# Retention's sample values by a transfer instead of a selector product, and layer norms that take the moments first

## The chip, the core and the metric

The kernel runs on one core of a Trainium2 chip as one program. Its time is the device time in microseconds (us), given as the median of several runs. The engines named below are TensorE (PE, with PEld for its weight loads), VectorE (DVE), ScalarE (ACT), GpSimd (POOL) and SyncE (SP). Every transfer between the chip's DRAM and its on-chip memory is issued by SP, in the order of the program, and is carried by the 16 DMA engines that all transfers share.

## The reference, cut to what matters

Two decoder layers work on one prompt (16 learned meta tokens and 256 tokens) and on 8 samples of one token each. In each layer three mixers (Mamba-2, HGRN2, retention) read one projection, their outputs are merged by gates, and layer norms and a SwiGLU follow. The parts that matter here are the retention step of the samples and the layer norm:

```
new_state = state * gamma(h) + k (outer) v        # per sample and head: 256 x 512
o         = q @ new_state
mu  = mean(x);  var = mean((x - mu)^2);  y = (x - mu) * rsqrt(var + eps) * g + b
```

There are 4 heads and 8 samples, so 32 such states in a layer and 64 in all. Each state is read from DRAM, updated and written back (512 KB each way).

## The kernel before

Features lie on the 128 partitions and the 280 tokens (272 of the prompt, 8 samples) along the free dimension. All large products go through blocks of 128 output features: `wblock` (L204) loads 512 KB of weights into one of 3 `raw` buffers, ACT rounds them to `wh`, and DVE computes the remainder `wl` (4 buffers each). 24 matmuls (L160, `large`) then make one block in PSUM tile `pp`. Small products (L169, `mm`) are placed between them: generators of the mixers are advanced one step by `tick()` twice in a block, so the order of the work on each engine is fixed when the program is built, and every engine runs its own queue in that order. SP's queue is one of these: a transfer that must wait holds up all those behind it.

The samples' retention is `ret_samples` (L753). The generator runs beside the later projections of its layer, one sample in a step. A step does the following:

- PE makes the output products of the sample before (`po<-st`, 8 matmuls).
- SP loads the state into one of 3 `st` buffers, and ACT multiplies it by gamma (L769).
- PE fetches the values: `vb` (L771) is a product of a selector column, broadcast over 128 columns, with `vhl`, which holds the samples' values as two rounded parts on 96 partitions. It puts the 512 values of sample b on all 128 partitions of a PSUM bank.
- DVE adds k times `vb` to the state in two instructions (`st<-vb`), and SP stores the state (L774).

Mamba and HGRN2 already hand their samples' values on in another way. They store them as rows in DRAM, and `everywhere` (L613) loads rows with a stride of 0 over the partitions, into tile `vh` (4 buffers, 256 KB a load).

A layer norm takes the sums by products with 1/1024 (`onesd`); `inv_std` then computes the inverse deviation, and `scaled` multiplies, applies gain and bias, and splits x into `px` tiles. `opening` (L228) starts the next projection: three blocks at once, which begin with those parts of x that are ready. `less(j)` subtracts the mean from quarter j of x. At the start `ln_input` does the same for the input, while the first weights arrive. The last norm writes the result, `yT`.

Of the kernel before, what the change touches and what calls it, by code (L numbers as in the profile page):

```python
# [8 lines left out]
F32 = mybir.dt.float32  # L9
# [6 lines left out]
P = 128  # L16
L = 2

OPEN = 3
# [69 lines left out]
def body(ctx: ExitStack, tc: tile.TileContext, a: dict):  # L89
# [113 lines left out]

    def wblock(src, nk):  # L204

        src_ = wraw.tile([P, RC, P], F32, tag="raw", name="raw")
        load(out=src_[:, :nk, :], in_=src)
        hi = whp.tile([P, RC, P], F32R, tag="wh", name="wh")
        lo = wlp.tile([P, RC, P], F32R, tag="wl", name="wl")
        with tc.high_priority(offset=boost):  # L210
            copy(hi[:, :nk, :], src_[:, :nk, :])
            ins = sub(lo[:, :nk, :], src_[:, :nk, :], f32(hi[:, :nk, :]))
        if fence:
            nosync(raw(ins), fence.pop())
        return hi, lo
# [9 lines left out]

    opened, norm_end = [], []

    def opening(srcs, c0):  # L228

        ps = [pp.tile([P, 512], F32, tag="pp", name="pp")[:, c0:T] for _ in srcs]  # L230
        ws = [wblock(src, KB) for src in srcs]
        for j in range(4):
            for p, w in zip(ps, ws):
                for k in (2 * j, 2 * j + 1):
                    for part in w:
                        large(p, part[:, k, :], blk(xhl[0], k)[:, c0:T], k == 0 and part is w[0], False)
        for j in range(3):
            for p, w in zip(ps, ws):
# [5 lines left out]
        opened.extend(ps)  # L244
        fence[:] = norm_end

# [110 lines left out]
    def scaled(x, rs, gk, bk, vec, less):  # L357
# [22 lines left out]
        with tc.high_priority(offset=AHEAD):  # L380
            vec(mul(x[0][:, 0, c], x[0][:, 0, c], rs))
            upper(0, V)
            vec(mul(x[0][:, 1, c], x[0][:, 1, c], rs))
            upper(1, S)
            times(1)
            upper(2, S)
# [33 lines left out]
    def ln_input(x):  # L420
# [4 lines left out]
        mm(m1, first, x[0][:, 0, :], True, True)  # L425
        for j in range(4):
            sub(x[j], x[j], b2(m1))
            sq = pair("pm")
            S.activation(sq, x[j], AF.Square)
            if j % 2:  # L430
                total = pair("pm")
                add(total, x[j - 1], x[j])
                for i in range(2):
                    ins = mm(mu, onesd, total[:, i, :], j == 1 and i == 0, j == 3 and i == 1)
            if j < 3:
                add(sq[:, 0, :], sq[:, 0, :], sq[:, 1, :])
                mm(m2, onesd, sq[:, 0, :], j == 0, False)
            else:
                for i in range(2):
                    ins = mm(m2, onesd, sq[:, i, :], False, i == 1)  # L440
        keep_warm(14, ins)
        rs = tt_()
        scaled(x, rs, "lnin_g", "lnin_b", *inv_std(rs, mu, m2, x))

    def inv_std(rs, mu, m2, x):
# [4 lines left out]
        def less(j):  # L450
            vec(sub(x[j][:, :, c], x[j][:, :, c], b2(mu)))

        with tc.high_priority(offset=AHEAD):
            S.activation(rs, mu, AF.Square)
            less(0)
            vec(sub(rs, m2, rs))
            vec(V.tensor_scalar(rs, rs, 0.0, None, ALU.max))
            rstd_of(rs, rs, 1.0, 0)
            less(1)
        return vec, less  # L460

    class Residual:
# [37 lines left out]
        def norm(self, gk, bk, out=None):  # L500
# [5 lines left out]
            for j in range(4):  # L506
                x = self.x[j]
                if j > 1:
                    less(j)
                vec(mul(x[:, :, c], x[:, :, c], b2(rs)))  # L510
                for i in range(2):
                    ins = affine(x[:, i, c], x[:, i, c], gk, bk, 2 * j + i, S if i else V)
                    if i == 0:
                        vec(ins)
                store(out=out[j], in_=x[:, :, c])
# [22 lines left out]
    V.tensor_copy(negb, negm)  # L538
    selb = cst.tile([P, 8], F32R, name="selb")
    V.tensor_copy(selb, small[:, 24:32])  # L540
    selh = cst.tile([P, 16], F32R, name="selh")
# [71 lines left out]
    def everywhere(rows, bb):  # L613

        vb = flat("vh")
        load(out=vb, in_=rows[2 * bb:2 * bb + 2, :].rearrange("b q -> (b q)").unsqueeze(0).to_broadcast([P, 512]))
        return vb
# [26 lines left out]
    def ret_mix(l, h, proj, res):  # L644
# [24 lines left out]

        vhl = flat("vh", dt=F32R)  # L670
        vt = []
        for t0, n in TOK:
# [3 lines left out]
            if n < P:  # L676
                copy(vhl[0:32], ps[0:32, :])
                sub(vhl[32:64], ps[0:32, :], f32(vhl[0:32]))
                V.tensor_copy(vhl[64:96], f32(vhl[0:32]))
            else:  # L680
                hi, lo = flat("pm", dt=F32R), flat("pm", dt=F32R)
# [39 lines left out]

        res += y, vhl, qk, final
        sq = []
# [28 lines left out]

    def ret_samples(l, h, y, vhl, qk, ready):  # L753
        gam = 1.0 - 2.0 ** (-5.0 - h)
# [9 lines left out]
        for b in range(NS):  # L764
            yield 1
            if b:
                products(b - 1)
            st = state(a["s_ret"][l, h, b], "p (i q) -> p i q", i=2)
            S.activation(st, st, AF.Copy, scale=gam)  # L769
            vb = vbt()  # L770
            mm(vb, selb[0:96, b:b + 1].to_broadcast([96, P]), vhl[0:96, :], True, True)  # L771
            for i in range(2):
# [881 lines left out]
```

## Time and profile before

| | us |
|---|---|
| median of 3 runs | 1899.39 (1896.95 to 1900.35) |
| profiled execution, its time | 1897.69 |
| profiled execution, its span | 1895.6 |
| PE busy | 1827.3 |
| DVE busy | 1353.2 |
| ACT busy | 1090.3 |

The span is what the trace covers of the profiled execution. Samples' retention lies at about 396 to 640 us in layer 0 and at 1340 to 1580 us in layer 1. The norms lie at the start, at about 750, 961 and 1682 us, and at the end. A tile's name in a row stands for all its buffers; `out<-in` says what an instruction writes and reads.

### The profile page before, as it was taken

How to read it: one execution, taken by the hardware profiler on the slowest of the kernel's cores; microseconds unless marked ns; L12 is line 12 of the kernel's file. 1: busy time of each engine (PE TensorE's matmuls, PEld its weight loads, DVE VectorE, ACT ScalarE, POOL GpSimd, SP SyncE). 2: the span in 40 equal slices, each digit the busy share in tenths (PEclk: the TensorE clock that was granted, in tenths of full speed). 3: DMA queues.
4: the chain of work that ended last, by engine and by line, in shares of the span. 5: the costliest groups of instructions: out<-in, count | busy, mean ns of one | idle time of the engine just before them, and what ended most of it. 6: DMA issues, size and time to landing. Idle time of an engine off the chain costs nothing.

```text
span 1895.6 us, 38951 instructions
## 1 busy us (share of the span) xinstructions
PE 1827.3 (96%) x15744; PEld 1702.4 (90%) x15744; DVE 1353.2 (71%) x2183; ACT 1090.3 (58%) x1861; POOL 374.6 (20%) x415
## 2 busy tenths in 40 slices
PE   8989999999999999999999889999999999999997
PEld 7987788899888999999999778888988999999997
DVE  7898879766755766655478979996767567666654
ACT  6686677545555544544366857775455556454443
POOL 2032424211011023000220333342110100221001
PEclk9999999999999999999999989999999999999998
DMA  6545655556788744555545356555667886545563
GB/s 208 184 141 199 214 203 175 199 203 224 244 282 285 278 167 147 176 170 173 170 139 184 112 198 226 186 192 204 204 227 263 296 306 229 181 149 189 180 175 103
DMA packets 114995, 378.42 MB, mean 200 GB/s; under 512 B 13056, under 2 KB 18560, under 8 KB 114816
## 3 DMA queue, kind: packets, MB, share of 16 engines
q1 hardware_dynamic: 114816, 375.94, 59.1%
q8 instruction: 124, 2.03, 0.4%
q14 instruction: 55, 0.45, 0.1%
HBM read 317.61 MB, written 58.28 MB: 198 GB/s over the span
## 4 chain that ended last, share of the span: by engine, by line
PE 78%; DVE 11%; ACT 4%; DMA 3%; issue 2%; POOL 2%; DVEq 0%; ACTq 0%; POOLq 0%; SPq 0%
PE pp L160 63%; PE mx L169 9%; PE po L169 2%; PE vb L169 2%; DVE wl L142 2%; DVE pm L142 2%; DMA st<-s_ret 1%; DVE pa L142 1%; POOL hpt L142 1%; DMA ret_s<-st 1%; DVE py L154 1%; PE mx L172 1%; ACT wh L139 1%; DVE st L154 1%; DVE py L142 1%
## 5 line engine op out<-in xcount | busy, mean ns | idle before, releaser
L160 PE MATMUL pp<-px,wh 128*128 128x280 f32 (+1 forms) x5504 | 1119.0, 295 | 11.9 <-ACT pa L1090 5.7
L160 PEld LDWEIGHTS pp<-px,wh 128*128 128x128 f32 x5504 | 889.0, 190 | 29.8 <-issue 14.8
L142 DVE TENSOR_TENSOR wl<-raw,wh 128x1024 fp32r<-128x1024 f32 (+1 forms) x472 | 590.7, 1253 | 331.8 <-ACT wh L139 327.6
L160 PE MATMUL pp<-px,wl 128*128 128x280 f32 (+1 forms) x2752 | 796.7, 291 | 0.0
L139 ACT ACTIVATE wh<-raw 128x1024 fp32r<-128x1024 f32 (+1 forms) x472 | 493.8, 1048 | 349.8 <-PE pp L160 239.3
L160 PEld LDWEIGHTS pp<-px,wl 128*128 128x128 f32 x2752 | 521.9, 190 | 4.3 <-issue 0.8
L160 PE MATMUL pp<-py,wh 128*128 128x280 f32 (+1 forms) x1984 | 383.4, 289 | 0.8 <-ACT py L139 0.8
L160 PEld LDWEIGHTS pp<-py,wh 128*128 128x128 f32 x1984 | 313.7, 188 | 3.8 <-ACT py L139 1.3
L160 PE MATMUL pp<-py,wl 128*128 128x280 f32 (+1 forms) x992 | 285.2, 288 | 0.0
L160 PEld LDWEIGHTS pp<-py,wl 128*128 128x128 f32 x992 | 186.6, 188 | 0.7
L142 POOL TENSOR_TENSOR pa<-pa 128x280 f32<-128x280 f32 (+3 forms) x56 | 75.2, 1353 | 362.3 <-DVE pa L142 257.1
L169 PE MATMUL mx<-pm 128*32 128x16 f32 (+8 forms) x1728 | 116.6, 231 | 8.2 <-POOL pm L142 6.9
L769 ACT ACTIVATE st<-st 128x1024 f32<-128x1024 f32 x64 | 67.8, 1059 | 94.9 <-DMA st<-s_ret 62.7
L169 PEld LDWEIGHTS mx<-pm 128*32 128x32 f32 (+2 forms) x1728 | 87.5, 131 | 29.6 <-POOL pm L142 7.5
L154 DVE SCALAR_TENSOR_TENSOR st<-vb,qks,st 128x512 f32<-128x512 f32 x128 | 91.2, 745 | 23.7 <-PE vb L169 23.2
L142 DVE TENSOR_TENSOR pm<-pm 128x64 f32<-128x64 f32 (+7 forms) x179 | 85.9, 502 | 14.5 <-ACT pm L736 8.4
L142 DVE TENSOR_TENSOR pa<-pa,pp 128x280 f32<-128x280 f32 (+1 forms) x152 | 65.9, 433 | 37.0 <-PE pp L160 25.3
L142 POOL TENSOR_TENSOR pa<-px 128x560 f32<-128x560 f32 (+1 forms) x16 | 25.4, 1586 | 305.0 <-DVE py L142 304.8
L132 ACT ACTIVATE pm<-pm 128x544 f32<-128x544 f32 (+4 forms) x112 | 58.0, 540 | 13.2 <-DVE pm L154 13.1
L132 ACT ACTIVATE pa<-pp 128x280 f32<-128x280 f32 (+1 forms) x124 | 47.3, 385 | 28.8 <-PE pp L160 28.7
L139 ACT ACTIVATE pa<-pp 128x280 f32<-128x280 f32 (+1 forms) x80 | 31.4, 392 | 39.7 <-PE pp L160 39.6
L154 DVE SCALAR_TENSOR_TENSOR st<-vh,qks,st 128x128 f32<-128x128 f32 x128 | 39.7, 370 | 19.5 <-POOL st L142 11.7
(252 smaller groups left out, 1871.9 us busy)
## 6 DMA issues: line engine op xcount, KB each, us to landing
raw<-w_in SPq DMA_DIRECT2D x256, 512.0 KB
raw<-w_ffn_in SPq DMA_DIRECT2D x88, 512.0 KB
st<-s_ret SPq DMA_DIRECT2D x64, 512.0 KB
ret_s<-st SPq DMA_DIRECT2D x64, 512.0 KB
vh<-rows SPq DMA_DIRECT2D x64, 256.0 KB
raw<-w_br_r SPq DMA_DIRECT2D x32, 512.0 KB
raw<-w_ffn_out SPq DMA_DIRECT2D x32, 512.0 KB
st<-s_ssm SPq DMA_DIRECT2D x16, 512.0 KB
```

What stands on the lines that cost most here:

```text
L132: ins = S.activation(out, in_, func, **kw)
L139: return S.activation(out, in_, AF.Copy)
L142: return e.tensor_tensor(out, x, y, op)
L154: return V.scalar_tensor_tensor(out, x, s, y, op0, op1)
L160: place[0] = raw(TE.matmul(out, lhsT, rhs, start=start, stop=stop, skip_group_check=True))
L169: return put(TE.matmul(out, lhsT, rhs, start=start, stop=stop, skip_group_check=True))
L172: return put(TE.transpose(out, x, ident))
L769: S.activation(st, st, AF.Copy, scale=gam)
```

## The change

A head's values of the samples are now copied on ACT from PSUM into two `pq` tiles and stored as 8 rows of 512 in DRAM (`vrows`, 2 buffers). In each step `everywhere` loads one row to all partitions, into the 4 `vh` buffers, and DVE reads it there. The selector product is gone. `vhl` stays for the prompt's products but moves to the tile `pb`, which has one buffer.

In the norms `less(0)` and `less(1)` move behind the computation of the variance: before, the DVE subtracted the mean from x[0] ahead of it. `ln_input` issues its steps in another order, loads the first three weight blocks there and ties two of their copies behind the last square (and one behind the inverse deviation). The last norm puts nearly all of its gain and bias on ACT.

```diff
@@ wblock
-            copy(hi[:, :nk, :], src_[:, :nk, :])
+            ins = copy(hi[:, :nk, :], src_[:, :nk, :])
+            if behind_ is not None:
+                nosync(raw(ins), raw(behind_))
@@ opening
-        ws = [wblock(src, KB) for src in srcs]
+        ws = ahead or [wblock(src, KB) for src in srcs]
@@ scaled
             upper(1, S)
+            less(1)
             times(1)
@@ ln_input
+        centre(0)
+        centre(1)
+        mean(0)
+        centre(2)
+        centre(3)
+        squares(0)
+        mean(1)
+        squares(1)
+        squares(2)
...
+        ahead.extend(wblock(a["w_in"][0, b], KB, last_sq) for b in range(OPEN - 1))
         keep_warm(14, ins)
...
+        how = inv_std(rs, mu, m2, x)
+        fence[:] = norm_end
+        ahead.append(wblock(a["w_in"][0, OPEN - 1], KB, run["ops"][-1]))
+        scaled(x, rs, "lnin_g", "lnin_b", *how)
@@ inv_std
             S.activation(rs, mu, AF.Square)
-            less(0)
             vec(sub(rs, m2, rs))
             vec(V.tensor_scalar(rs, rs, 0.0, None, ALU.max))
             rstd_of(rs, rs, 1.0, 0)
-            less(1)
+            norm_end[:] = [less(0)]
@@ Residual.norm
-                if j > 1:
-                    less(j)
                 vec(mul(x[:, :, c], x[:, :, c], b2(rs)))
+                if j < 3:
+                    less(j + 1)
                 for i in range(2):
-                    ins = affine(x[:, i, c], x[:, i, c], gk, bk, 2 * j + i, S if i else V)
...
+                    ins = affine(x[:, i, c], x[:, i, c], gk, bk, 2 * j + i, V if i == 0 and j == 3 else S)
@@ everywhere
-        load(out=vb, in_=rows[2 * bb:2 * bb + 2, :].rearrange("b q -> (b q)").unsqueeze(0).to_broadcast([P, 512]))
+        n = 512 // rows.shape[1]
+        load(out=vb, in_=rows[n * bb:n * bb + n, :].rearrange("b q -> (b q)").unsqueeze(0).to_broadcast([P, 512]))
@@ ret_mix
-        vhl = flat("vh", dt=F32R)
+        vhl = flat("pb", dt=F32R)
+        rows = dr.tile([NS, 512], F32, tag="vrows", name="vrows")
...
+                for i in range(2):
+                    vs, c = flat("pq", 256), slice(256 * i, 256 * i + 256)
+                    copy(vs[0:32], ps[0:32, c])
+                    store(out=rows[:, c], in_=vs[24:32])
@@ ret_samples
             st = state(a["s_ret"][l, h, b], "p (i q) -> p i q", i=2)
+            vb = everywhere(rows, b)
             S.activation(st, st, AF.Copy, scale=gam)
-            vb = vbt()
-            mm(vb, selb[0:96, b:b + 1].to_broadcast([96, P]), vhl[0:96, :], True, True)
```

The scheduler places the instructions anew. On SP's queue, in the last head of layer 0, one finds before (`st` loads from `s_ret`, `raw` are weight blocks, `ret_s` the stores of states; the numbers name single buffers' contents):

```order
L587 DMA st_7393<-s_ret 128x1024
L207 DMA raw_7424<-w_in 128x1024
L774 DMA ret_s<-st_7202 128x1024
L207 DMA raw_7478<-w_in 128x1024
L587 DMA st_7458<-s_ret 128x1024
L207 DMA raw_7511<-w_in 128x1024
L774 DMA ret_s<-st_7258 128x1024
L207 DMA raw_7555<-w_in 128x1024
L587 DMA st_7545<-s_ret 128x1024
```

And at the same head now (`vh` loads the values of a sample from `vrows`):

```order
L605 DMA st_7419<-s_ret 128x1024
L635 DMA vh_7421<-vrows_6021 128x512
L207 DMA raw_7450<-w_in 128x1024
L605 DMA st_7484<-s_ret 128x1024
L635 DMA vh_7486<-vrows_6021 128x512
L798 DMA ret_s<-st_7419 128x1024
L207 DMA raw_7504<-w_in 128x1024
L207 DMA raw_7537<-w_in 128x1024
L798 DMA ret_s<-st_7484 128x1024
L605 DMA st_7571<-s_ret 128x1024
L635 DMA vh_7573<-vrows_6021 128x512
```

Before, a state's store stood two loads behind its own load; now it stands one load behind it, and a values' load stands behind each state's load.

On DVE, in the norm at the start (`x0` is x, `tt` the variance and then the inverse deviation, `mx_107` the mean, `lbt`, `negb`, `selb`, `selh` and `wdt` are constants), there stood before:

```order
L142 TENSOR_TENSOR wl_241<-raw_238,wh_240 128x1024
L142 TENSOR_TENSOR x0_87<-x0_87,mx_107 128x560
L142 TENSOR_TENSOR tt_153<-mx_108,tt_153 128x280
L538 CAST negb_209<-negm_203 128x288
L457 TENSOR_SCALAR tt_153<-tt_153 128x280
L142 TENSOR_TENSOR x0_88<-x0_88,mx_107 128x560
L142 TENSOR_TENSOR wl_247<-raw_244,wh_246 128x1024
L142 TENSOR_TENSOR wl_253<-raw_250,wh_252 128x1024
L142 TENSOR_TENSOR x0_87<-x0_87,tt_153 128x280
L878 CAST wdt_230<-tt_353 128x8x16
L343 TENSOR_SCALAR px_162<-x0_87,par_95 128x280
```

And now:

```order
L142 TENSOR_TENSOR wl_147<-raw_144,wh_146 128x1024
L556 CAST identb_225<-ident_215 128x128
L142 TENSOR_TENSOR tt_165<-mx_108,tt_165 128x280
L142 TENSOR_TENSOR lbt_244<-par_95,lbt_244 128x8 x2
L479 TENSOR_SCALAR tt_165<-tt_165 128x280
L142 TENSOR_TENSOR x0_87<-x0_87,mx_107 128x560
L558 CAST negb_227<-negm_221 128x288
L560 CAST selh_229<-small_219 128x16
L142 TENSOR_TENSOR x0_87<-x0_87,tt_165 128x280
L346 TENSOR_SCALAR px_179<-x0_87,par_95 128x280
L142 TENSOR_TENSOR x0_87<-x0_87,tt_165 128x280
L142 TENSOR_TENSOR x0_88<-x0_88,mx_107 128x560
```

Two `wl` stood between the variance and the product of x[0] with the inverse deviation. Now they stand ahead of the variance, and the third (`wl_176`) follows on the last row shown, ahead of the product for x[1].

## Rows read from the trace of the kernel before

**Rows 1.** the page: busy time by engine, then the chain that ended last, by line
```profile
PE 1827.3 (96%) x15744; PEld 1702.4 (90%) x15744; DVE 1353.2 (71%) x2183; ACT 1090.3 (58%) x1861; POOL 374.6 (20%) x415
...
PE pp L160 63%; PE mx L169 9%; PE po L169 2%; PE vb L169 2%; DVE wl L142 2%; DVE pm L142 2%; DMA st<-s_ret 1%; DVE pa L142 1%; POOL hpt L142 1%; DMA ret_s<-st 1%; DVE py L154 1%; PE mx L172 1%; ACT wh L139 1%; DVE st L154 1%; DVE py L142 1%
```

**Rows 2.** windows, retention's samples: us; PE, PEld, DVE, ACT, POOL; PEclk, DMA share, GB/s
```profile
396.00:500.00 104.00, 102.54 (x791) 93.22 (x791) 70.99 (x107) 57.36 (x97) 10.60 (x13) 1.00 0.66 226
500.00:640.00 140.00, 137.26 (x1088) 124.41 (x1088) 85.47 (x107) 75.11 (x102) 14.88 (x10) 1.00 0.83 289
1340.00:1440.00 100.00, 97.86 (x769) 89.10 (x768) 67.61 (x105) 52.58 (x90) 12.29 (x16) 1.00 0.65 221
1440.00:1580.00 140.00, 139.80 (x1157) 126.32 (x1157) 92.41 (x117) 81.22 (x113) 13.56 (x10) 1.00 0.87 301
```

**Rows 3.** groups by form, window 500 to 640: count, busy us, mean ns
```profile
L169 PE MATMUL vb<-vh,selb 96*128 96x512 f32 x20 | 9.8, 488 | 0.0
```

**Rows 4.** the same group, window 1440 to 1580
```profile
L169 PE MATMUL vb<-vh,selb 96*128 96x512 f32 x21 | 10.3, 488 | 0.0
```

**Rows 5.** chain in order of time, window 500 to 545: start us, us, what
```profile
511.08 0.42 PE vb L169
```

**Rows 6.** timeline of PE, window 510 to 512: start us, us, engine, line, what
```profile
511.01 0.49 PE L169 MATMUL vb<-vh,selb 96*128 96x512 f32 x1
...
511.35 0.29 PE L160 MATMUL pp<-px,wh 128*128 128x280 f32 x1
```

**Rows 7.** the page's DMA queues: packets, MB, share of 16 engines' span
```profile
q1 hardware_dynamic: 114816, 375.94, 59.1%
```

**Rows 8.** windows: the mixers before retention, then two 20 us stretches with DMA busiest
```profile
95.00:390.00 295.00, 277.88 (x2884) 244.26 (x2883) 248.84 (x494) 199.29 (x431) 97.87 (x98) 0.98 0.56 188
...
620.00:640.00 20.00, 20.00 (x161) 18.17 (x161) 16.04 (x22) 12.30 (x17) 0.00 (x0) 1.00 0.94 346
...
1460.00:1480.00 20.00, 20.00 (x169) 18.22 (x169) 11.70 (x10) 11.59 (x18) 6.02 (x5) 1.00 0.94 327
```

**Rows 9.** chain again, the wait at 525 us
```profile
525.22 6.41 DMA ret_s<-st
...
531.70 2.62 DMA st<-s_ret
```

**Rows 10.** waits of the DMA queue: us in total, times, longest
```profile
SPq L587 <- DMA ret_s<-st: 102.4, 44, 5.8
...
SPq L616 <- DVE st L154: 37.3, 13, 5.7
...
SPq L616 <- DMA rows<-pq: 10.7, 8, 2.2
```

**Rows 11.** groups by form, whole span: count, busy us, mean ns, idle before
```profile
L154 DVE SCALAR_TENSOR_TENSOR st<-vb,qks,st 128x512 f32<-128x512 f32 x128 | 91.2, 745 | 23.7 <-PE vb L169 23.2
...
L154 DVE SCALAR_TENSOR_TENSOR st<-vh,qks,st 128x128 f32<-128x128 f32 x128 | 39.7, 370 | 19.5 <-POOL st L142 11.7 <-DMA raw<-w_in 4.2 <-DMA st<-s_ssm 3.6
...
L154 DVE SCALAR_TENSOR_TENSOR st<-vh,py,st 128x256 f32<-128x256 f32 x64 | 30.1, 501 | 0.3
...
L139 ACT ACTIVATE pq<-mx 128x256 f32<-128x256 f32 x24 | 8.9, 372 | 4.2 <-PE mx L169 3.8
...
L169 PE MATMUL vb<-vh,selb 96*128 96x512 f32 x64 | 31.4, 490 | 0.0
```

**Rows 12.** timeline, the norm at the start
```profile
16.38 2.35 DVE L142 TENSOR_TENSOR wl<-raw,wh 128x1024 fp32r<-128x1024 f32 x2
...
18.65 0.44 DVE L142 TENSOR_TENSOR x<-x,tt 128x280 f32<-128x280 f32 x1
...
25.17 0.39 PE L160 MATMUL pp<-px,wh 128*128 128x280 f32 x1 [0.24 <-ACT px L342]
```

**Rows 13.** timeline, the norm at the end
```profile
1883.78 0.70 DVE L142 TENSOR_TENSOR pa<-pa,mx 128x528 f32<-128x528 f32 x1 [0.93 <-ACT tt L454]
...
1890.88 0.71 DVE L142 TENSOR_TENSOR pa<-pa,tt 128x528 f32<-128x528 f32 x1
```

More of the change, by code (lines that the diff above doesn't have):

```diff
@@ L201, in body, with wblock @@
     fence, hold = [], []
-    def wblock(src, nk):
+    def wblock(src, nk, behind_=None):
         src_ = wraw.tile([P, RC, P], F32, tag="raw", name="raw")
@@ L224, in project @@
                 tick()
-    opened, norm_end = [], []
+    opened, norm_end, ahead = [], [], []
     def opening(srcs, c0):
         ps = [pp.tile([P, 512], F32, tag="pp", name="pp")[:, c0:T] for _ in srcs]
-        ws = [wblock(src, KB) for src in srcs]
+        ws = ahead or [wblock(src, KB) for src in srcs]
         for j in range(4):
@@ L244, in opening @@
         opened.extend(ps)
+        ahead.clear()
         fence[:] = norm_end
@@ L425, in ln_input, with centre, mean, squares @@
         mm(m1, first, x[0][:, 0, :], True, True)
[L426 to L440, printed above, removed]
+        vec = chained()
+        sq, total = pairs("pm", 4), pairs("pm", 2)
+        squared = []
+        def centre(j):
+            vec(sub(x[j], x[j], b2(m1)))
+            squared.append(S.activation(sq[j], x[j], AF.Square))
+        def mean(j):
+            vec(add(total[j], x[2 * j], x[2 * j + 1]))
+            for i in range(2):
+                mm(mu, onesd, total[j][:, i, :], i + j == 0, i + j == 2)
+        def squares(j):
+            vec(add(sq[j][:, 0, :], sq[j][:, 0, :], sq[j][:, 1, :]))
+            mm(m2, onesd, sq[j][:, 0, :], j == 0, False)
+        centre(0)
[7 more added lines that the diff above has]
+        squares(2)
+        for i in range(2):
+            ins = mm(m2, onesd, sq[3][:, i, :], False, i == 1)
+        last_sq = squared[-1]
+        ahead.extend(wblock(a["w_in"][0, b], KB, last_sq) for b in range(OPEN - 1))
         keep_warm(14, ins)
         rs = tt_()
-        scaled(x, rs, "lnin_g", "lnin_b", *inv_std(rs, mu, m2, x))
+        how = inv_std(rs, mu, m2, x)
+        fence[:] = norm_end
+        ahead.append(wblock(a["w_in"][0, OPEN - 1], KB, run["ops"][-1]))
+        scaled(x, rs, "lnin_g", "lnin_b", *how)
     def inv_std(rs, mu, m2, x):
@@ L450, in less @@
         def less(j):
-            vec(sub(x[j][:, :, c], x[j][:, :, c], b2(mu)))
+            return vec(sub(x[j][:, :, c], x[j][:, :, c], b2(mu)))
         with tc.high_priority(offset=AHEAD):
             S.activation(rs, mu, AF.Square)
-            less(0)
             vec(sub(rs, m2, rs))
@@ L507, in norm @@
                 x = self.x[j]
-                if j > 1:
-                    less(j)
                 vec(mul(x[:, :, c], x[:, :, c], b2(rs)))
+                if j < 3:
+                    less(j + 1)
                 for i in range(2):
-                    ins = affine(x[:, i, c], x[:, i, c], gk, bk, 2 * j + i, S if i else V)
-                    if i == 0:
-                        vec(ins)
+                    ins = affine(x[:, i, c], x[:, i, c], gk, bk, 2 * j + i, V if i == 0 and j == 3 else S)
                 store(out=out[j], in_=x[:, :, c])
@@ L538, in body @@
     V.tensor_copy(negb, negm)
-    selb = cst.tile([P, 8], F32R, name="selb")
-    V.tensor_copy(selb, small[:, 24:32])
     selh = cst.tile([P, 16], F32R, name="selh")
@@ L679, in ret_mix @@
                 V.tensor_copy(vhl[64:96], f32(vhl[0:32]))
+                for i in range(2):
+                    vs, c = flat("pq", 256), slice(256 * i, 256 * i + 256)
+                    copy(vs[0:32], ps[0:32, c])
+                    store(out=rows[:, c], in_=vs[24:32])
             else:
@@ L720, in final @@
             store(out=a["ret_p"][l, h, i], in_=so)
-        res += y, vhl, qk, final
+        res += y, rows, qk, final
         sq = []
@@ L751, in ret_mix, with ret_samples @@
             mul(y[j][:, :, 0:TP], y[j][:, :, 0:TP], rs[:, 0:TP].unsqueeze(1).to_broadcast([P, 2, TP]))
-    def ret_samples(l, h, y, vhl, qk, ready):
+    def ret_samples(l, h, y, rows, qk, ready):
         gam = 1.0 - 2.0 ** (-5.0 - h)
```

## The prediction

> **What bounds the kernel now.** I read the page first: PE is busy for 96% of the span, and the chain that ended last lies on PE for most of its length, above all in the large products of L160 [rows 1]. An instruction that leaves PE's queue therefore shortens the program by its slot, as long as nothing else becomes late. Then I read the windows of the stage that changes. In the samples' retention PE idles for 1.46 us of 104, 2.74 of 140, 2.14 of 100 and 0.20 of 140, in all 6.5 us [rows 2]. The reader is to look at the DMA share in the same rows as well: 0.66 and 0.65 in the first part of each layer's stage, 0.83 and 0.87 in the second. PE is full everywhere, but the transfers are nearly full in the second parts only. That decides the forecast.
>
> **The selector products.** 64 of them go. In the later windows there are 20 and 21 [rows 3, 4], which leaves 23 of 64 for the earlier ones. In the chain one costs 0.42 us [rows 5]; on PE's timeline the next large product begins 0.34 us after it [rows 6]. I take 0.42, because the chain also holds what is lost at the change of operands; 0.34 is the other end. The whole is 64 x 0.42 = 26.9 us, or 21.8. [...]
>
> **The transfers that come in their place.** 64 loads of 262144 bytes. The queue's packets take 59.1% of 1895.6 us for 375.94 MB [rows 7], 2.98 us per MB with all 16 engines, so 0.78 us for one load. From both sides: at the rate of the row of 620 to 640 (346 GB/s at a share of 0.94, so 368 at full share) it is 0.71 us. In the mixers before retention, where half of the existing loads of this kind lie, the share of 0.56 makes 165 us for 55.5 MB; if all but their 8.4 MB moved at the rate of the window of 500 to 640 (2.87 us per MB), 30 us would be left for 32 loads, 0.93 each [rows 2, 8]. I take 0.78, the mean over nearly all bytes.
>
> In the first parts the transfers have room: 0.66 x 104 + 12 x 0.78 = 78 of 104 us. There PE's saving counts in full: 23 x 0.42 = 9.7 us.
>
> In the second parts I set PE's need against that of the transfers. Layer 0: PE would need 140 - 20 x 0.42 - 2.7 = 128.9 us; the transfers need 0.83 x 140 + 20 x 0.78 = 131.8 us at full share. Layer 1: PE 140 - 21 x 0.42 - 0.2 = 131.0; transfers 0.87 x 140 + 21 x 0.78 = 138.2. In both the transfers end last, so this stage loses part of what PE gives. I take 131.8 and 138.2, a gain of 8.2 + 1.8 = 10.0 us: with more transfers than PE can wait for, something is always outstanding, and the three `st` buffers and the weights in hand let them reach a little over the edges. The bounds are a share of 0.94, the highest 20 us rows [rows 8], which makes 140.2 and 147.0, a loss of 7.2; and all hidden, a gain of 11.1 + 9.0 = 20.1.
>
> **The waits for states.** Some of PE's idle time comes from the recycling of the three state buffers. The chain has one such place: a store of 6.41 us, then the load of 2.62 into the same buffer [rows 9]. SP waited for such stores 44 times, 102.4 us in all [rows 10]. Now DVE can update a state as soon as state and values have landed; it no longer waits for PE's place in the order, and by the order the store stands one load earlier. So the buffer is written back while PE has not yet read it, and that wait should nearly go. What is late next is the load itself. Of the 3.6 us of idle time in the first parts I count half, 1.8 us; none and all are the ends. In the second parts the idle time is in the sums above.
>
> **Other costs of the move.** DVE now reads the values from on-chip memory and not from PSUM. With PSUM 512 elements take 745 ns; the same instruction with `vh` takes 370 for 128 and 501 for 256, so 131 per 128 and some 763 for 512 [rows 11]. 128 x 18 ns = 2.3 us on DVE, which is busy for 71 of 104 and 85 of 140 us [rows 2]: nothing. If DVE's cover were gone, 2.3 us. ACT gets 16 copies of 32 x 256 from PSUM; the nearest row, 128 x 256, takes 372 ns [rows 11], 6 us over both layers, beside an ACT that is busy for half of the stage: nothing, or 6 us without that cover. SP waits for the rows to land before it may load them. Mamba and HGRN2 pay 10.7 us for 8 such waits, 1.34 each [rows 10]; by the order only the first head of a layer loads at once behind its store, so 2.7 us on SP, behind which weight loads stand. Three `raw` buffers and four of `wh` and `wl` lie between them and PE, at 24 matmuls a block; nothing, 2.7 at most. `vhl` in the single `pb` buffer: a head's transposes must follow the last products of the head before, and the generator runs the heads one after the other anyway: nothing, and no bound above a few tenths a head.
>
> **The norms.** At the start two `wl` (2.35 us) kept DVE from the product with the inverse deviation, which began at 18.65 [rows 12]; now they stand ahead of the variance, under PE's moments. The first large products come some 2 us sooner. But the third `wl` and `less(1)` now stand ahead of the product for x[1], 1.2 and 0.7 us, and PE's last wait of the opening, which ended at 25.17, is for the last parts of x [rows 12]. I take 0.5, between 0 and 2.0. In the three inner norms the variance starts 0.7 us sooner (the length of a `less`, [rows 13]), and `less(1)` takes as much back ahead of the product for x[1]; what ends last there is again the last part of x. I take 0, between +0.7 and -0.7 each. At the end there is no next projection. What ends last there is DVE, from `less(0)` at 1883.78 to the last product, which ends at 1891.59 [rows 13]: `less(0)` no longer delays the variance (0.70), and three instructions of gain and bias leave DVE. I take 1.0, between 0.5 and 1.5. Together 1.5 us.
>
> **The sum.** 9.7 + 1.8 + 10.0 + 1.5 = 23.0 us. The profiled execution took 1897.69 us, of which the span is 1895.6; 1897.69 - 23.0 = 1874.7. The median of the runs shown is 1899.39, 1.7 above the profiled one, so I forecast 1876.4 and say 1876.
>
> **The rivals.**
>
> *All transfers are hidden.* PE gives back 26.9, all 6.5 us of idle time and 3.0 in the norms, 36.4 in all: 1863. For it: shares of a microsecond or two reach 1, so the engines can be driven harder than 0.94, and loads of values can run ahead by four buffers. Against it: with 20 more loads the second part of layer 0 needs more than PE leaves. [...] Chance 0.22.
>
> *The transfers take back nearly all.* At a share of 0.94 the second parts lose 7.2; the first parts gain 9.7, the norms 1.5, and the waits for states stay: 1899.4 - 4.0 = 1895. For it: 0.94 is the highest row that I have. Against it: no row has a demand above 1. Chance 0.17, its range from 1888 to 1902. Here belongs also that the change doesn't do what it says: the product goes, but PE waits in the same place for a state whose update waits for the values' load.
>
> *SP's queue becomes the bound: slower.* A values' load must wait until DVE has freed a `vh` buffer, and everything behind it on SP waits too, weights and states. The loads of this kind that exist cost SP 37.3 us in 13 waits [rows 10], 0.58 for each of 64. Another 64 would cost 37; where the transfers have no slack (41 of the 64) that is 24 us that can't be made up. With the loss of 7.2 above, and 9.7 + 1.5 gained: 1899.4 + 20 = 1919. It decides as soon as the second parts together lose more than the 11.2 gained elsewhere. Against it: the order loads values up to four samples ahead, when the update that frees the buffer lies long behind. Chance 0.12.
>
> **How the numbers follow.** My forecast has a chance of 0.49, its own range 1868 to 1888. A change within 0.2% (3.8 us) can't be told from none. All cases below 1895.6 are faster: 0.49 + 0.22 and half of the second rival, 0.79. The rest of the second makes no difference, 0.09. Slower is 0.12. The range runs from the lower end of the first rival to the second rival's middle and a little over, 1860 to 1899; outside lie the third rival and small tails.
>
> **What would show it.** The group of 64 products is gone from PE. The DMA share in the second parts is 0.93 or more, and PE idles there, released through a state, a weight copy or a values' load; in the first parts PE idles no more than before, and these parts are some 5 us shorter each. SP's waits for `ret_s` stores nearly vanish. Large products begin before 18 us, but PE's last wait in that opening still ends at about 24.7. The forecast is wrong if the share in the second parts stays below 0.9 with PE full (first rival), or if PE idles while the DMA engines do (third).

## The result and the profile after

The changed kernel takes 1913.16 us (1911.33 to 1914.41, 4 runs), the kernel before 1899.37: a ratio of 1.0079, interval 1.0060 to 1.0097. It is slower, and the forecast was 1876. The profiled execution took 1914.41 us, its span is 1912.3.

The page, busy time and chain [rows 1], and the queue [rows 7]:

```profile
PE 1824.0 (95%) x15680; PEld 1697.4 (89%) x15680; DVE 1355.8 (71%) x2179; ACT 1101.2 (58%) x1880; POOL 373.9 (20%) x415
...
q1 hardware_dynamic: 124288, 392.85, 61.2%
...
PE pp L160 59%; PE mx L169 9%; DMA st<-s_ret 3%; DMA vh<-vrows 2%; DVE wl L142 2%; DVE st L154 2%; DVE pm L142 2%; PE po L169 2%; DVE pa L142 1%; DMA raw<-w_in 1%; POOL hpt L142 1%; ACT wh L139 1%; PE mx L172 1%; DVE py L154 1%; DVE py L142 1%
```

64 products are gone, yet the chain has less PE and more transfers: states, values and weights. The same four windows as in [rows 2] (us; PE, PEld, DVE, ACT, POOL; PEclk, DMA share, GB/s):

```profile
396.00:500.00 104.00, 102.72 (x803) 93.70 (x802) 70.46 (x107) 58.91 (x101) 10.99 (x13) 1.00 0.72 245
500.00:640.00 140.00, 132.57 (x1043) 119.89 (x1043) 82.80 (x103) 75.02 (x101) 14.88 (x10) 0.98 0.88 299
1340.00:1440.00 100.00, 97.92 (x780) 89.59 (x780) 67.71 (x103) 55.50 (x97) 13.21 (x17) 1.00 0.68 232
1440.00:1580.00 140.00, 126.65 (x1020) 113.31 (x1019) 80.34 (x99) 73.88 (x101) 14.18 (x10) 0.98 0.85 293
```

In the second parts PE idles for 7.4 and 13.4 us (before 2.7 and 0.2), and the DMA share is 0.88 and 0.85: PE waits, and the DMA engines are not full either. GB/s in the last row is lower than before (293 against 301) although there is more to carry.

To see where the time went I count large products. Both traces hold 11,232 of them in the same order, 24 to a block, so the start of each block's last product can be compared. Four stretches hold nearly all of the difference: first parts (after block 75 to 96 in layer 0, 307 to 331 in layer 1) and second parts (96 to 133, 331 to 367):

| us | forecast | before | after | difference |
|---|---|---|---|---|
| first parts, 11 and 13 products less | gain 11.5 | 103.6 + 114.2 | 100.7 + 111.2 | gain 5.9 |
| second parts, 20 and 19 products less | gain 10.0 | 139.2 + 126.8 | 142.4 + 147.0 | loss 23.4 |
| five norms | gain 1.5 | | | gain 0.9 |
| span | gain 23.0 | 1895.6 | 1912.3 | loss 16.7 |

What SP waited for, over the whole span [rows 10]:

```profile
SPq L798 <- DVE st L154: 205.3, 63, 6.8
...
SPq L635 <- DVE st L154: 34.0, 13, 5.7
...
SPq L704 <- ACT pq L139: 23.2, 8, 6.2
...
SPq L635 <- DMA vrows<-pq: 2.0, 2, 1.0
```

The wait of state loads for `ret_s` stores (102.4) is gone, as foretold. In its place SP waits at the stores themselves, for DVE's update: 205.3 us, where the kernel before had 55.3. In the stretch 1440 to 1600 the queue shows what that displaces. Before, then after:

```profile
SPq L207 <- DVE wl L142: 50.6, 27, 3.6
SPq L587 <- DMA ret_s<-st: 32.0, 16, 4.4
SPq L774 <- DVE st L154: 13.8, 12, 1.6
```

```profile
SPq L798 <- DVE st L154: 84.6, 20, 6.8
SPq L207 <- DVE wl L142: 18.1, 10, 3.8
```

A wait of SP for `wl` is a good sign: weights are so far ahead that no `raw` buffer is free. It falls from 50.6 to 18.1. What PE then waits for is weights; over the whole span the changed kernel has these two waits, 24.0 us together, and the kernel before has none for `wl` or `wh`:

```profile
PE pp L160 <- DVE wl L142: 13.2, 15, 1.8
...
PE pp L160 <- ACT wh L139: 10.8, 9, 2.8
```

One sample of layer 1, on SP's timeline and then in the chain (start, us, what):

```profile
1500.04 0.34 SPq L798 DMA_DIRECT2D ret_s<-st  x1
1500.48 0.39 SPq L605 DMA_DIRECT2D st<-s_ret  x1
1500.92 0.83 SPq L635 DMA_DIRECT2D vh<-vrows  x1
1501.80 1.27 SPq L207 DMA_DIRECT2D raw<-w_br_h  x2
1503.17 1.88 SPq L605 DMA_DIRECT2D st<-s_ret  x1
1510.89 0.34 SPq L798 DMA_DIRECT2D ret_s<-st  x1
```

```profile
1500.48 6.89 DMA st<-s_ret
...
1507.39 1.07 ACT st L795
...
1509.07 0.75 DVE st L154
...
1510.16 0.67 DVE st L154
```

From 1505.05 to 1510.89 SP issues nothing: the next entry is the store, the store waits for the update, the update for a state that took 6.89 us. Weights stand behind the store. The DMA engines still carry what was issued before, 311 GB/s at a share of 0.97 from 1505 to 1510; from 1510 to 1512, when that runs out, it is 203 GB/s at 0.52. The update can also wait for the values: between 1440 and 1600 DVE waited 18.6 us for `vh` to land ahead of updates, and 13.0 us for ACT's product of the state.

### The profile page after: what moved, and what is told of

It is laid out like the page before. It is cut to its first block, busy times and chain, and to the rows that moved or that the text cites. A ratio compares the mean times of both kernels' runs of the same rounds, so it can differ in the third digit from the quotient of the medians.

```text
span 1912.3 us, 38905 instructions
## 1 busy us (share of the span) xinstructions
PE 1824.0 (95%) x15680; PEld 1697.4 (89%) x15680; DVE 1355.8 (71%) x2179; ACT 1101.2 (58%) x1880; POOL 373.9 (20%) x415
## 4 chain that ended last, share of the span: by engine, by line
PE 71%; DVE 11%; DMA 7%; ACT 6%; issue 2%; POOL 2%; SPq 0%; DVEq 0%; ACTq 0%; POOLq 0%
PE pp L160 59%; PE mx L169 9%; DMA st<-s_ret 3%; DMA vh<-vrows 2%; DVE wl L142 2%; DVE st L154 2%; DVE pm L142 2%; PE po L169 2%; DVE pa L142 1%; DMA raw<-w_in 1%; POOL hpt L142 1%; ACT wh L139 1%; PE mx L172 1%; DVE py L154 1%; DVE py L142 1%
## 5 line engine op out<-in xcount | busy, mean ns | idle before, releaser
L160 PE MATMUL pp<-py,wh 128*128 128x280 f32 (+1 forms) x1984 | 388.5, 292 | 5.0 <-ACT wh L139 4.2
L154 DVE SCALAR_TENSOR_TENSOR st<-vh,qks,st 128x128 f32<-128x128 f32 (+1 forms) x256 | 140.5, 595 | 107.0 <-ACT st L795 43.9
L142 POOL TENSOR_TENSOR st<-st,hfc 128x1024 f32<-128x1024 f32 x16 | 34.2, 2134 | 89.7 <-DMA st<-s_hgrn 54.5
```

Of the source, the lines that this page charges most:

```text
L142: return e.tensor_tensor(out, x, y, op)
L154: return V.scalar_tensor_tensor(out, x, s, y, op0, op1)
L160: place[0] = raw(TE.matmul(out, lhsT, rhs, start=start, stop=stop, skip_group_check=True))
```

## The experiments

The medians and ratios, each against the kernel before on the same chip, and the four stretches of each profiled execution. Single executions differ by some us, so a stretch shows a loss of 5 us well and one of 1 us not: "before", "norms alone" and "before, 4 states", which all keep the selector product, have 126.8, 129.5 and 128.6 us in the last column.

The expectations use four names: theory A, an entry that waits holds up SP's queue; B, DVE stands at an update and holds up the weights' remainders; C, the 16 engines can't carry the added bytes; D, they could, but waits leave them without work.

| kernel | median us | ratio (95% interval) | first 0 | second 0 | first 1 | second 1 |
|---|---|---|---|---|---|---|
| before | 1899.4 | | 103.6 | 139.2 | 114.2 | 126.8 |
| after | 1913.2 | 1.0079 (1.0060 to 1.0097) | 100.7 | 142.4 | 111.2 | 147.0 |
| norms alone | 1897.9 | 0.9998 (0.9978 to 1.0017) | 103.3 | 138.1 | 115.7 | 129.5 |
| retention alone | 1920.3 | 1.0101 (1.0060 to 1.0142) | 100.1 | 144.8 | 111.5 | 146.5 |
| update tied | 1912.5 | 1.0067 (1.0047 to 1.0087) | 102.2 | 140.8 | 111.3 | 137.2 |
| store later | 1909.0 | 1.0045 (1.0017 to 1.0074) | 106.0 | 139.9 | 115.5 | 138.7 |
| store on POOL | 1917.5 | 1.0092 (1.0066 to 1.0118) | 104.2 | 143.6 | 115.5 | 138.3 |
| before + idle loads | 1921.6 | 1.0117 (1.0090 to 1.0145) | 103.9 | 144.7 | 118.8 | 139.0 |
| a quarter of the bytes | 1898.8 | 0.9990 (0.9972 to 1.0007) | 100.1 | 135.5 | 108.9 | 136.3 |
| a quarter, tied | 1894.4 | 0.9977 (0.9960 to 0.9993) | 101.6 | 132.2 | 110.7 | 131.6 |
| other buffers | 1922.1 | 1.0101 (1.0084 to 1.0119) | 100.4 | 134.6 | 112.9 | 139.5 |
| before, other buffers | 1929.5 | 1.0141 (1.0119 to 1.0163) | 103.4 | 141.2 | 113.7 | 128.7 |
| tied, other buffers | 1923.4 | 1.0119 (1.0096 to 1.0142) | 100.9 | 139.2 | 112.2 | 138.4 |
| store later, 4 states | 1898.2 | 0.9997 (0.9980 to 1.0014) | 103.3 | 138.6 | 113.3 | 127.2 |
| before, 4 states | 1900.8 | 1.0008 (0.9990 to 1.0025) | 103.0 | 139.8 | 113.6 | 128.6 |
| hybrid | 1892.0 | 0.9957 (0.9941 to 0.9972) | 99.2 | 138.3 | 110.3 | 130.2 |
| hybrid, tied | 1896.0 | 0.9980 (0.9965 to 0.9994) | 100.3 | 136.6 | 114.9 | 129.4 |
| hybrid, 4 states | 1891.0 | 0.9965 (0.9951 to 0.9980) | 100.1 | 136.9 | 109.9 | 129.8 |

**The two halves.** Norms alone keep the selector product (the retention part of the diff is taken back); retention alone keeps the old norms.

> The changed norms alone; retention keeps the selector product. If the loss sits in the norms, this kernel is slower than before, by up to 14 us (1913). If it sits in retention's loads, as the two traces laid block by block say (start -0.3, each inner norm +0.15 to +0.3, end -1.2 us), it ends at 1898 to 1899, and no retention group of its trace differs from before. My forecast for the norms was a gain of 1.5.

> Retention's loads alone; the norms as before. If the norms took part in the loss, 1905 or less; if all of it is retention's, 1914, with the same two stretches as in the changed kernel where PE loses 7 and 21 us, behind weight copies.

The norms are worth nothing that can be measured, and the loss is retention's.

**The place of update and store.** Three edits of the changed kernel that keep all bytes. Tied:

```diff
-                stt(st[:, i, :], vb, qk[:, 2 + i, b:b + 1], st[:, i, :], ALU.mult, ALU.add)
+                put(stt(st[:, i, :], vb, qk[:, 2 + i, b:b + 1], st[:, i, :], ALU.mult, ALU.add))
```

> The changed kernel, all its transfers kept; only the two updates of a state on DVE are tied, in the order alone, behind the large product that PE issued last, as the selector product was. By the order the store of a state then stands 4.2 weight blocks behind its load (before 5.0, changed kernel 2.0), and the update 1.6 blocks after it in place of -0.4. Theory A (SP holds back weights at a store that waits for an update): the 205 us of waits at ret_s stores fall below 100, PE's idle time behind weight copies (24 us) goes, 1880 to 1890. Theory B (DVE stands in order at an update and holds back the weights' remainders): also 1880 to 1890. Theory C (the 16 engines can't carry 16.8 MB more): no better than 1905.

Store later (the old state's store is issued in the next step, behind that step's loads):

```diff
+            old, st = st, state(a["s_ret"][l, h, b], "p (i q) -> p i q", i=2)
             vb = everywhere(rows, b)
+            if b:
+                put(store(out=a["ret_s"][l, h, b - 1], in_=old))
```

> The changed kernel; only the store of a state is issued one sample later and tied there, in the order alone, 4.8 weight blocks behind its load in place of 2.0. The update on DVE stays where the change put it (-0.4 blocks). Theory A (SP's wait at the store): the waits at ret_s stores fall below 100 us, 1880 to 1892, though state loads may again wait for a buffer to be written back, as they did before (102 us). Theory B (DVE's place): stays at 1908 to 1914, with SP's waits at stores short and PE idle behind wl all the same. Theory C (bandwidth): no better than 1905, the DMA share above 0.93 in the second parts.

And the store on another queue, `G.dma_start` in place of `store`:

> The changed kernel, with the 64 stores of states issued by POOL in place of SP; DVE's order and all bytes stay. So far: putting the update or the store back later in the order (two kernels) brought 1909 to 1912 from 1914, so the store's wait on SP alone didn't hold most of the loss. Theory A (a waiting entry of SP's queue, whichever it is: after the store was moved, SP waited 79 us for a values' buffer and 128 us for a state's buffer instead): without stores in the queue most waits go, 1885 to 1895. Theory C (bytes): 1905 or more, DMA share 0.93 or more in the second parts.

None gives back half of the loss (the best, 1.0045 from 1.0079, with intervals that overlap), so theories A and B don't hold in the form in which they were put. The wait moves on instead. SP's largest waits around retention in store later, and in store on POOL:

```profile
SPq L605 <- DMA ret_s<-st: 128.5, 51, 6.3
SPq L635 <- DVE st L154: 79.2, 33, 5.9
```

```profile
SPq L635 <- DVE st L154: 160.1, 56, 6.6
```

**The bytes.** Idle loads: the kernel before, product kept, plus in each step

```diff
+            idle = wk.tile([P, 512], F32, tag="vh", bufs=4, name="idle")
+            load(out=idle, in_=a["s_ret"][l, h, b, 0:1, 0, :].to_broadcast([P, 512]))
```

> The kernel before, selector product kept, with 64 loads of 262144 bytes added to SP's queue (one row of a state to 128 partitions) that nothing reads. Bytes alone, no update that waits for them; by the order the store stands 4.6 blocks behind its load. Theory C (bytes): the second parts need 140 to 147 us and more at the shares that these engines reach, 1906 to 1915. Theory A: same as before, 1899 to 1902.

A quarter: `load(out=vb[:, 0:128], ...)`, and the update reads these 128 columns four times.

> The changed kernel, but a values' load brings 128 of the 512 columns only, and the update uses them four times (the new states and outputs of the samples are therefore others). Order, number of transfers and all waits stay, 12.6 of the 16.8 MB go. Theory C (bytes): 64 x 0.59 us of the engines' time goes, the two stretches where PE lost 7 and 21 us vanish, 1882 to 1890. Theory A (waits in the order): the update still waits for a state load and SP at the store behind it, 1905 or more, SP's waits at the stores near 200 us.

> Both at once: a values' load of 128 columns used four times (as in the quarter run, so the samples' states and outputs are others), and the update tied behind PE's large product. The quarter run alone brought 1899, the tie alone 1912. If the place of update and store still cost some 10 us once the bytes are gone (theory A beside C), this one ends at 1884 to 1891. If the tie is worth nothing, 1896 to 1900.

64 loads that nobody reads cost 22 us (1921.64 - 1899.35), more than the whole change lost; PE's saving is not yet taken off here. This is not bytes alone: the idle loads take turns in the `vh` buffers, for which SP waited 35.9 us, and SP's waits at the stores rose from 55.3 to 123.6 us. With a quarter of the bytes most of the changed kernel's loss goes, but 1898.8 lies between what the two theories expected, and theory A's waits did stay: SP waits 181.2 us at the stores. So the sum of these waits does not measure the loss. In layer 1's second part 136.3 us are left, 9.5 over the kernel before. The tie gains 4 us more there, which the intervals (0.9972 to 1.0007 and 0.9960 to 0.9993) do not separate. So the added transfers are the cause; but at what limit, the engines' rate or something else?

**Transfers alone.** Two kernels of SP's queue only, no arithmetic and no outputs. The core of a group, with `raw`, `state`, `values` each a load into its own pool and `away` a store:

```
raw(p); held.append(state(p))
if with_values: values(p)
if len(held) > 2: away(held.pop(0))
raw(p)
```

A state's store stands two loads behind its own load, as in the kernel before; in the changed kernel it stands one behind. Nothing updates the state in between.

> Transfers alone, no arithmetic and no outputs: SP issues, one behind the other, 80 weight loads of 512 KB; 120 values' loads of 256 KB from one row; then three times 36 groups of two weights, one state load and the store of an older state, the first time without and then with a values' load, with 26 buffers in all, and the third time with the kernel's 3, 3 and 4. Theory C in its strong form (the engines can't carry the mix faster than the second parts show): the mix moves at no more than 320 GB/s even with many buffers, and the packets' share is at 0.9 or more. Theory D (the engines could, but waits leave them without work): 340 GB/s or more with many buffers, and the third mix shows what 10 buffers allow. A values' load costs 0.78 us of the engines if the mean price of all bytes holds for it, 0.71 to 0.93 by the bounds.

> Transfers alone again, no arithmetic and no outputs: 36 groups of two weights, a state load and an older state's store, first without values' loads at 3 and 3 buffers, then with values' loads at raw, st, vh = 3, 3, 4; 4, 3, 4; 3, 4, 4; 4, 4, 4. Theory D: the rate rises with the count, from some 310 GB/s at 3, 3, 4 to 340 or more at 4, 4, 4; and without values' loads it is at 300 to 320 too, so that every added load lengthens the group by its bytes at that rate, 0.8 us. Theory C: all five near 310.

Windows of the first burst (POOL, PEclk, DMA share, GB/s): weights; values' loads; the mix without and with values on 26 buffers; the mix on 3, 3 and 4:

```profile
20.00:90.00 70.00, 0.00 (x0) 1.00 1.03 410
110.00:170.00 60.00, 0.00 (x0) 1.00 1.04 373
220.00:350.00 130.00, 0.00 (x0) 1.00 1.03 420
390.00:560.00 170.00, 0.00 (x0) 1.00 1.03 415
600.00:820.00 220.00, 0.00 (x0) 1.00 0.92 311
```

And of the second: without values on 3 and 3 buffers; then with values on raw, st, vh = 3, 3, 4; 4, 3, 4; 3, 4, 4; 4, 4, 4:

```profile
20.00:220.00 200.00, 0.00 (x0) 1.00 0.90 315
260.00:480.00 220.00, 0.00 (x0) 1.00 0.92 309
520.00:740.00 220.00, 0.00 (x0) 1.00 0.93 315
800.00:960.00 160.00, 0.00 (x0) 1.00 1.03 416
1000.00:1160.00 160.00, 0.00 (x0) 1.00 1.03 418
```

In this burst the state buffers decide: three give 309 to 315 GB/s, a fourth 416, a fourth weight buffer alone 315. (A share of 1.03 shows that this count is more than plain busy time.) With three, SP waits at the state loads until the store of the state that held the buffer has landed, 136.9 us in 29 waits in the third window:

```profile
SPq L103 <- DMA sink<-st: 136.9, 29, 6.1
```

A group takes 6.5 us without and 7.5 with a values' load (36 groups in 235.2 and 269.8 us), and 5.7 with four state buffers (205.8). A sample in the kernels' second part of layer 1 takes 126.8 / 19 = 6.7 us before and 147.0 / 19 = 7.7 after. The paces are close, but the match does not show that the round of state buffers set the kernel's pace before: PE idled there for 0.2 us of 140 [rows 2], so PE's own work set the 6.7, and the round's 6.5 lay just below it. In the burst a values' load lengthens the round by about 1 us, which would lift it above PE's work. That the changed kernel's 7.7 is this round is inferred from the match, and tested next.

**Buffers in the kernel.** Other buffers: `wraw` 4, `stp` 4, `whp` 3, `wlp` 3 in the same memory.

> The changed kernel with other buffer counts in the same memory: raw 4 (3), st 4 (3), wh 3 (4), wl 3 (4). The burst with 26 buffers carried the second parts' mix at 415 GB/s, with the kernel's 3, 3 and 4 at some 310, the rate that the second parts show. Theory D (too few transfers can be under way): the second parts, 142 and 147 us now, fall towards what PE needs without the product, 133 and 121, so 1880 to 1890, at over 330 GB/s there. Theory C (a limit of the engines for this mix): no better than 1908.

> The kernel before with the same buffer counts, as a control. Its second parts are bound by PE for all but 3 us, so theory D has it at 1894 to 1900; if the counts help wherever weights flow, it gains as much as the changed kernel does, and the two stay 14 us apart.

> The same buffer counts, and the update tied behind PE's large product (1912 without the counts). Theory D: the store's early place, which holds SP until the update is done, costs what the quarter runs show between them (1899 and 1894), so 2 to 6 us less than the run without the tie: 1876 to 1886. Theory C: no better than 1905.

The changed kernel's second parts come down by 7.8 and 7.5 us, those of the control don't. But the changed counts cost 28 us in the control, mostly outside retention, so the whole is slower, and theory D's times for all three failed. The three `wh` and `wl` are the likely reason, as a fourth state buffer costs the control nothing clear of noise below (1.0008); no run has them alone. Then the fourth state buffer with the weights' buffers left alone (`pm` 11, `pq` 6 make room), on the kernel with the later store:

> The changed kernel with the store of a state one sample later (1909 so far, where SP then waited 128 us for state buffers to be written back) and a fourth state buffer; the memory comes from pm (11 for 12) and pq (6 for 7), the weights' buffers are untouched. In the burst the fourth state buffer alone took the mix from some 310 to 416 GB/s. Theory D: SP's waits at state loads go, the second parts (142 and 147 us in the changed kernel) come down to PE's need of some 133 and 121, 1878 to 1890. If the second parts stay at 137 or more each, the fourth buffer is not what holds them, 1900 to 1910.

> Control: the kernel before with the same four state buffers, pm 11 and pq 6. PE idles 6.5 us in its retention stage, of which the fourth buffer can give back a part, and fewer pm and pq buffers can cost something in the mixers: 1893 to 1902.

All of the changed kernel's bytes, and 1898.2 in place of 1913.2; the control does not gain. Of the 15.0 us the later store alone brings 4.2 (1909.0) and the fourth buffer 10.8. The fourth buffer with the store in its early place was not run without other counts. Layer 1's second part falls from 147.0 by way of 138.7 to 127.2. The window 1450 to 1520, in the changed kernel and then in this one:

```profile
1450.00:1520.00 70.00, 65.53 (x545) 58.75 (x543) 38.98 (x47) 36.28 (x50) 10.99 (x8) 1.00 0.86 300
```

```profile
1450.00:1520.00 70.00, 70.00 (x596) 63.93 (x595) 42.94 (x51) 41.15 (x55) 11.88 (x8) 1.00 0.95 349
```

PE is full and the same engines carry 349 GB/s. The whole second part of layer 1, again the changed kernel and then this one:

```profile
1450.20:1597.23 147.03, 129.81 (x1031) 116.00 (x1030) 82.69 (x101) 73.01 (x98) 14.18 (x10) 0.97 0.85 289
```

```profile
1453.98:1581.22 127.24, 122.85 (x1030) 111.08 (x1030) 83.01 (x102) 72.80 (x99) 15.87 (x10) 1.00 0.91 330
```

PE's idle time falls from 17.2 to 4.4 us. The rest of the 19.8 us, 7.0, is PE's busy time for the same work; the mean granted clock of 0.97 in place of 1.00 makes up to 4.4 us of that (0.03 x 147, an estimate). So in layer 1 it was not the engines' rate: it was the round of state buffers and waits in SP's queue, and beside them the lower clock (0.97 against 1.00). The expectation for the whole (1878 to 1890) failed all the same: this part stays 6 us above the 121 expected, and layer 0's second part (138.6) and the first parts (103.3 and 113.3) did not come down to the forecast; SP still waits 83.3 us for states to be written back and 81.0 for values' buffers in this kernel. What holds those stretches stays open.

**A version that beats both.** Hybrid: transfer for heads 0 and 1, most of whose steps lie in the first parts (DMA share 0.72 and 0.68 in the changed kernel), product for heads 2 and 3.

```diff
+            if h < 2:
                 vb = everywhere(rows, b)
             S.activation(st, st, AF.Copy, scale=gam)
+            if not (h < 2):
+                vb = vbt()
+                mm(vb, selb[0:96, b:b + 1].to_broadcast([96, P]), vhl[0:96, :], True, True)
```

> The changed kernel with the values by transfer for heads 0 and 1 of each layer and by the selector product, as before, for heads 2 and 3. Block by block the changed kernel gained up to 6.5 us in layer 0 and 4.7 in layer 1 ahead of the stretches where it lost. If the loss lies where the transfers are dense (theory C), this one keeps half to all of that and loses nothing: 1890 to 1895. If the order loses time wherever a values' load stands (theory A), 1898 to 1905.

> Heads 0 and 1 by transfer, heads 2 and 3 by the product (1892 so far), with the update tied behind PE's large product as well. In the first parts the transfers have room, so the tie has little to give back there: 1888 to 1893. If the early place of the update is itself worth something where there is room (states go back sooner), slower: 1893 to 1897.

> Heads 0 and 1 by transfer, 2 and 3 by the product (1892), with the four state buffers, pm 11 and pq 6. Its second parts (138 and 130 us) come down to PE's need there, some 134 and 121 to 124: 1882 to 1888. If the buffers cost as much elsewhere, 1890 to 1895.

1892.0 us, 0.43% faster than the kernel before. The tie brought nothing more (0.9980), nor did the fourth state buffer (0.9965), now that most of the dense parts carry no values; its second parts stayed at 136.9 and 129.8 us, where 134 and 121 to 124 were expected.

## Why the prediction was wrong

**The step that failed** is the sum for the second parts: "In both the transfers end last [...] I take 131.8 and 138.2." It priced a transfer by its time on 16 engines and let the engines be full. They can be (416 GB/s in the burst), but were not with three state buffers behind one queue in order (309 to 315). Where the sum gave a gain of 10.0, there was a loss of 23.4, of which 20.2 in layer 1. The bounds erred alike: even at a share of 0.94 I allowed a loss of 7.2. The reason I gave, that "something is always outstanding", does not hold: SP stands still for 5.8 us at a store, and at the end of that the engines run out (a share of 0.52 from 1510 to 1512).

**The clock stands nowhere in the sum.** It took PE's work after the change as that before less the products. In layer 1's second part the mean granted clock fell to 0.97, and the same work took PE 129.8 us where it takes 122.9 with the fourth state buffer at 1.00; up to 4.4 of these 7.0 us are clock by the estimate above.

**The share misled.** I read 0.94 as nearly full and 346 GB/s as nearly the rate. The burst shows 311 GB/s at a share of 0.92 and 415 at 1.03: by these the same bytes are counted as 19% more busy time (0.92 / 311 against 1.03 / 415) when fewer buffers feed the engines, and the share says little of what is left. The 368 GB/s that I worked out for a full share is no limit either: the burst carried 410 to 420 (weights, and the mixes with enough buffers; values' loads alone had 373). The price of one load was right where nothing waits: 120 in 87.3 us, 0.73 each (forecast 0.78).

**The waits for states** went as said and came back in another place. I noted that the store stands one load earlier and counted that as a gain; I did not ask what the store itself would then wait for, with the update's values and state only just loaded. That is the question for every entry that moves forward in a queue.

**The product's slot** was mis-sized: 0.42 from the chain, where 0.33 is right; the loss at a change of operands, for which I took the larger value, no row shows. In the kernel before, eight products `po` are followed by `vb` 0.57 us after their start and by a large product 0.34 later [rows 6]; in the changed kernel the large product follows at once. Before, then after:

```profile
510.44 0.64 PE L169 MATMUL po<-st,qd 128*32 128x256 f32 x8
```

```profile
585.19 0.64 PE L169 MATMUL po<-st,qd 128*32 128x256 f32 x8
585.76 0.40 PE L160 MATMUL pp<-py,wh 128*128 128x280 f32 x1
```

Over the steps with eight `po` and nothing else but `vb` between two large products, the median from the one to the next falls from 1.123 to 0.790 us. 24 products in the first parts are 7.9 us, of which 5.9 were kept; the waits there gave 0.2 of the 1.8 forecast (in the windows of [rows 2] PE idled 3.6 us before and 3.4 now).

**The third rival** had the right side and nearly the time (1919), at a chance of 0.12, but another place: the wait for `vh` buffers that it named did not grow (34.0 us in 13 waits, before 37.3 in 13). It appeared only when the store was moved out of the way (79.2 and 160.1 us). Its sign was the right one: PE idles while the DMA engines do (from 1510 to 1512 PE is busy for 0.75 of 2 us, at a DMA share of 0.52).

**The rest held.** The rows' landing cost SP 2.0 us (forecast 2.7); not foreseen were 23.2 us in which the row stores wait for ACT's copies. The update's mean is 816 ns against the 763 I gave it, but that comes from ten of the 128 (last section); the median is 747, before 744. I put it at nothing because DVE had room; in the sample above, though, two updates lie on the chain that SP's store waits for. DVE by form [rows 11]:

```profile
L154 DVE SCALAR_TENSOR_TENSOR st<-vh,qks,st 128x512 f32<-128x512 f32 x128 | 100.2, 816 | 89.2 <-ACT st L795 43.9 <-DMA vh<-vrows 32.0 <-DMA ret_p<-pm 5.0
```

In the norms, the first large products came 2 us sooner and the last wait hardly moved [rows 12]; the end gained 1.2 us, the start 0.3, the inner three lost 0.6 together:

```profile
17.74 0.37 PE L160 MATMUL pp<-px,wh 128*128 128x280 f32 x1
...
24.91 0.39 PE L160 MATMUL pp<-px,wh 128*128 128x280 f32 x1 [0.24 <-ACT px L345]
```

## What to carry to other kernels

Price a transfer that is put into a full stage by the round it joins, not by its bytes alone (here 1.0 us of the round in the burst, where the load alone took 0.73): count the buffers of the chain load, update, store, and what the queue in front of the next load waits for. When an entry of an in-order queue moves forward, ask what it will wait for there and what stands behind it (SP's waits at the stores went from 55.3 to 205.3 us). A DMA share of 0.9 is not proof of full engines; a burst of the same mix with more buffers tells (309 GB/s at 0.92, and 416 with one state buffer more). A mean that has moved is not yet a slower instruction: look at the median and at the outliers (the update's mean 816 ns, its median 747).

## What the runs showed of the hardware that was not expected

One buffer more for one kind of transfer, 4 in place of 3 for the states, changed the rate of the whole mix from 309 to 416 GB/s, at shares of 0.92 and 1.03.

A lower clock came beside idle time of PE. In the changed kernel PE waited 2.84 us until 577.10 and 0.66 until 578.35, and the granted clock was 0.50 from 577 to 583 us; two large products took 0.67 us there, where two took 0.42 later:

```profile
578.00:583.00 5.00, 4.65 (x20) 4.65 (x21) 3.75 (x5) 2.47 (x3) 1.38 (x1) 0.50 0.69 231
```

```profile
577.10 0.60 PE L160 MATMUL pp<-py,wh 128*128 128x280 f32 x1 [2.84 <-ACT wh L139]
578.35 0.60 PE L160 MATMUL pp<-py,wl 128*128 128x280 f32 x1 [0.66 <-DVE wl L142]
578.75 0.67 PE L160 MATMUL pp<-py,wh 128*128 128x280 f32 x2
...
583.42 0.42 PE L160 MATMUL pp<-py,wh 128*128 128x280 f32 x2
```

In the 140 us windows of the second parts the mean clock was 0.98 where it had been 1.00. That such waits bring the clock down is not shown: in the kernel before, PE waited 1.70 us until 537.98, and the clock was 1.00 from 536 to 545.

The update reads the values from on-chip memory as fast as it did from PSUM (median 747 and 744 ns), except beside one instruction of POOL. Ten of the 128 updates take 1.27 to 1.89 us. Each of the ten starts while POOL runs an instruction `pa<-pa`, which reads and writes on-chip memory too, and ends 547 to 556 ns after that instruction's end, as if it had waited for it. In the rows below the first of two updates takes 747 ns and the second 1893:

```profile
504.13 2.56 DVE L154 SCALAR_TENSOR_TENSOR st<-vh,qks,st 128x512 f32<-128x512 f32 x2
```

```profile
504.27 1.86 POOL L142 TENSOR_TENSOR pa<-pa 128x560 f32<-128x560 f32 x1 [34.44 <-ACT pa L132]
```

With PSUM as the source none of the 128 takes over 753 ns, though six start beside such an instruction.
